# Layer boundaries that leave the trunk divided by a per-token factor, with another chain of norms; layer B's weight remainders on VectorE alone; layer C's cache loads spread out

## The chip, the cores and the metric

One of the eight cores of one Trainium2 chip. The metric is the device time of the program in microseconds (us); the shown figure is the median of three runs.

## The reference

One inference step of a four-layer encoder for 336 tokens: 64 frames of a running stream and 272 (16 meta tokens and 256 frames) of a new one. Each layer is

```
x <- x + rmsnorm(mixer(rmsnorm(x, norm_pre)), norm_post)
rmsnorm(x, g) = x * rsqrt(mean(x*x) + 1e-6) * g
```

with D_MODEL = 1024, and the mixers are A = HGRN2 recurrence, B = RG-LRU (causal convolution, two block-diagonal gates, a linear recurrence), C = latent attention with a cache of 528 rows, D = a 31-tap convolution module. Each mixer has an input projection from 1024, a SiLU gate of width 2048, and an output projection from 2048 to 1024. The outputs are the 336 rows of x after layer D and the new states of the mixers.

## The kernel before, in words

Everything lies transposed: features on the 128 partitions, the 336 tokens along the free axis, so x is 8 slices of 128x336. Every weight matrix is read once, in groups of up to 128x1024 float32, by class `Weights`: a DMA on SP's queue into one of three `wraw` buffers, a rounded part `whi` made by ScalarE (L321), and the remainder `wlo = wraw - whi` (L333) made by VectorE (DVE), or by GpSimd (POOL) for the groups that stand in `PRM["lo"]`. Of these, 26 belong to layer B (10 `bg`, 8 `bx`, 4 `bw`, and the 4 `bo1` that exist) and 38 to layer D. There are five buffers for the pairs `whi`, `wlo`. A product is three matmuls (`mm3`): whi with the rounded activations, whi with their remainder, wlo with the rounded ones.

The order of the work is the order of the Python program: each engine runs its own instructions in that order (`manual_schedule`), and the lists in `PRM` say which step of which unit comes next. `PRM["b"]` is layer B's list of steps with a lag each: a unit n is 256 of the 2048 channels, with two x tiles (`x0`, `x1`), two gate tiles (`g0`, `g1`), a convolution for each x tile (`conv0`, `conv1`, L942 and L944), `split` (rounded part and remainder of the convolved tile), `gate` (the two block-diagonal products, tile `gacc`), `decay` (L978 to L980, with a POOL square), `mult` (L985, L986), `root` (L990 to L994) and `recur` (the scan L1000, the gating L1004 and L1005, and the split into `oh`, `ol`, L415 and L416). What is left after the last g or x tile is handed out over the 16 slices of the output projection by `PRM["bt"]`.

`outproj` runs a layer's end. Its first phase goes over the 16 slices of `oh`, `ol` into MPAR accumulators (2 in A and C, 4 in B, 6 in D), its second makes the rest of the eight output slices one by one (`bacc`). `evac` takes each: the square (sums `s`), the slice times norm_post (`yg`), its square (sums `q`), and x times yg (sums `p`); POOL also makes the sums of x squared (`xsq`, L544 and L546). Four float32 matmuls with a matrix of ones (`Ss`, `Sq`, `Sp`, `Sx`) sum over the partitions. From Ss comes r = rsqrt(mean y^2 + eps) (`rstd`, L422 Ln and L423 Exp); POOL multiplies the eight `yg` slices by r (L587); the sum of squares of the new x is Sx + r (2 Sp + r Sq) (L589 to L592), and another Ln and Exp give the next layer's factor `rn`. `first_tiles` then goes over the eight slices: `upd` adds yg to x (L596), `scale` makes u = x * norm_pre * rn (L460), ScalarE rounds it to `uh` (L466) and DVE makes `ul` (L471), while TensorE runs the next layer's first four tiles (`hacc`), three matmuls for each of four tiles in every slice. `w.ahead()` and `w.get()` move the weight pipeline on.

Layer C's head (L1085 to L1093) issues ten loads (RoPE tables, pair mask, cache) on ScalarE's queue, and then evacuates four q and two kv tiles (`raw_tile`, L1119 to L1123), with POOL adding the squares.

In layer D's output projection (`ready`, L1606 to L1625) DVE normalises a slice, POOL multiplies it with its gate (L1613), ScalarE rounds it and DVE makes the remainder `ol`, two to four slices ahead of TensorE.

Of the kernel before, what the change touches and what calls it, by code (L numbers as in the profile page):

```python
# [18 lines left out]
D = 1024  # L19
# [332 lines left out]
class Trunk:  # L352
# [14 lines left out]

    def start(self):
# [61 lines left out]
    def first_norm(self):  # L430
# [5 lines left out]
        sq0 = self.nrm.tile([128, NT], F32, name="sst")  # L436
# [5 lines left out]
        self.mm(ss[:, :NT], self.ones, sq0, True, True)  # L442
        self.w.ahead()
        return self.rstd(ss[:, :NT], D)

    def first_tiles(self, i, r, upd=None):
# [5 lines left out]
        order = [(k, j) for k in range(KD) for j in range(4)]  # L452
        if upd is None:
            upd = lambda k: None
            order.sort(key=lambda z: max(2 * z[0], 3 * z[1]))
        us = {}
# [34 lines left out]
    def outproj(self, i, layer, ready, close):  # L491
# [20 lines left out]
        with ExitStack() as st:  # L512
# [29 lines left out]
            def xsq(m):  # L542
                q = new("x", m)
                G.tensor_tensor(q, self.x[:, m], self.x[:, m], op=OP.mult)  # L544
                if m:
                    G.tensor_tensor(sums["x"], sums["x"], q, op=OP.add)  # L546
# [1125 lines left out]
```

## Time and profile before

| | |
|---|---|
| runs shown | 1369.55, 1371.46, 1374.95 us (median 1371.46) |
| profiled execution | 1373.4 us; span from the first to the last instruction 1371.3 us |
| mean granted TensorE clock | 0.968 of full |
| busy in the span | TensorE 92%, weight loads 87%, DVE 70%, ScalarE 60%, POOL 34% |
| layer A, B, C, D by their first tiles | 0 to 403, 403 to 662, 662 to 1046, 1046 to 1371 us |

Times in rows are counted from the start of the span. A matmul row starts when its data may enter the array, and neighbours overlap; the distance of two starts is what one costs. L390 is the line of every matmul, so its rows are told apart by their tiles. PEld is the weight load, ACTq and POOLq the queue of an engine. "idle before" with an arrow names what ended the wait.

### The profile page before, as it was taken

To read this page: it belongs to the slowest core of one execution; us is meant where nothing else is said; L and a number is where in the kernel's file an instruction comes from. 1 tells how busy PE (TensorE), PEld (TensorE's weight loads), DVE (VectorE), ACT (ScalarE), POOL (GpSimd) and SP (SyncE) were. 2 spreads that over 40 slices of the span, in tenths; PEclk is the share of its full clock that TensorE was granted. 3 is DMA by queue.
4 is the path that set the end of the run, shared out by engine and by line. 5 is a ranking of instruction groups with operands and counts; after the bars stand their busy time and mean duration, and the time that the engine had idled before them with its cause. 6 is when DMAs were issued, how large, how long until landed. Compare 5 with 4: busy or idle time off the path is not lost.

```text
span 1371.3 us, 21204 instructions
## 1 busy us (share of the span) xinstructions
PE 1267.3 (92%) x8016; PEld 1197.1 (87%) x8016; DVE 959.6 (70%) x1683; ACT 817.6 (60%) x1554; POOL 460.4 (34%) x452
## 2 busy tenths in 40 slices
PE   5999999999979998789789999998897999999996
PEld 5999999999969988789779998887796899888895
DVE  5676666667667989876665555554856699989783
ACT  4677766666535766655364444444543878777663
POOL 0000000002245534452240000000404599999783
PEclk9999999999989999999899999999998999999998
DMA  5433334333423333234342322131242232333251
GB/s 196 142 120 109 111 120 131 111 109 108 154 93 108 109 123 112 104 123 147 110 155 76 113 92 98 63 105 50 77 144 79 93 108 98 103 116 101 95 166 41
DMA packets 48422, 151.28 MB, mean 110 GB/s; under 512 B 6432, under 2 KB 12016, under 8 KB 48320
## 3 DMA queue, kind: packets, MB, share of 16 engines
q1 hardware_dynamic: 44880, 142.70, 31.8%
q0 software_dynamic: 1392, 4.63, 1.1%
q10 hardware_dynamic: 2048, 2.60, 0.6%
q8 instruction: 63, 1.03, 0.3%
q14 instruction: 39, 0.32, 0.1%
HBM read 145.45 MB, written 4.46 MB: 109 GB/s over the span
## 4 chain that ended last, share of the span: by engine, by line
PE 59%; DVE 15%; ACT 8%; POOL 5%; issue 5%; DMA 3%; ACTq 0%; POOLq 0%; SPq 0%; DVEq 0%
PE acc L390 32%; PE bacc L390 9%; DVE xc L944 3%; POOL gp L1481 3%; PE o L390 3%; PE cv L390 3%; PE hacc L390 2%; DMA wraw<-in_wts_dram 2%; DVE wlo L333 2%; PE y L390 2%; PE sp L390 2%; ACT whi L321 2%; ACT Pp L1349 2%; PE ss L390 2%; POOL wlo L333 1%
## 5 line engine op out<-in xcount | busy, mean ns | idle before, releaser
L390 PE MATMUL acc<-uh,wlo 128*128 128x336 f32 x1208 | 385.7, 319 | 11.7 <-DVE wlo L333 7.0
L390 PE MATMUL acc<-uh,whi 128*128 128x336 f32 x1208 | 393.7, 326 | 1.1 <-ACT vv L879 1.1
L390 PE MATMUL acc<-ul,whi 128*128 128x336 f32 x1208 | 384.3, 318 | 0.0
L321 ACT ACTIVATE whi<-wraw 128x1024 fp32r<-128x1024 f32 (+2 forms) x267 | 274.1, 1028 | 108.6 <-DMA wraw<-in_wts_dram 59.2
L333 DVE TENSOR_TENSOR wlo<-wraw,whi 128x1024 fp32r<-128x1024 f32 (+2 forms) x203 | 257.6, 1281 | 38.8 <-ACT whi L321 33.8
L390 PEld LDWEIGHTS acc<-uh,wlo 128*128 128x128 f32 x1208 | 228.7, 189 | 13.6 <-DVE wlo L333 7.9
L390 PEld LDWEIGHTS acc<-uh,whi 128*128 128x128 f32 x1208 | 229.5, 190 | 3.7 <-ACT vv L879 1.6
L390 PEld LDWEIGHTS acc<-ul,whi 128*128 128x128 f32 x1208 | 229.8, 190 | 2.1
L333 POOL TENSOR_TENSOR wlo<-wraw,whi 128x1024 fp32r<-128x1024 f32 (+1 forms) x64 | 155.5, 2434 | 115.8 <-DVE sump L522 74.3
L1489 DVE SCALAR_TENSOR_TENSOR cv<-dext,dw,cv 128x366 f32<-128x366 f32 x280 | 146.2, 602 | 2.0 <-POOL gp L1481 1.4
L1481 POOL TENSOR_TENSOR gp<-gp,gq 128x366 f32<-128x366 f32 x109 | 115.8, 1063 | 27.8 <-ACT gq L1480 21.3
L544 POOL TENSOR_TENSOR sumx<-x 128x336 f32<-128x336 f32 x3 | 2.8, 949 | 326.6 <-PE x L773 326.6
L390 PE MATMUL bacc<-oh,wlo 128*128 128x336 f32 x288 | 91.4, 317 | 1.0 <-DVE wlo L333 1.0
L390 PE MATMUL bacc<-oh,whi 128*128 128x336 f32 x288 | 92.2, 320 | 0.0
L390 PE MATMUL bacc<-ol,whi 128*128 128x336 f32 x288 | 91.1, 316 | 0.0
L1480 ACT ACTIVATE gq<-dext,dw 128x366 f32<-128x366 f32 x109 | 61.8, 598 | 25.8 <-POOL gp L1481 25.4
L1198 POOL DMA_DIRECT2D uv<-in_wts_dram x8 | 5.8, 720 | 199.3 <-DVE sg L1106 116.0
L390 PE MATMUL acc<-oh,whi 128*128 128x336 f32 x192 | 63.6, 331 | 9.2 <-DVE sgb L1015 6.8
L390 PE MATMUL acc<-ol,whi 128*128 128x336 f32 x192 | 63.3, 330 | 3.5 <-DVE ol L416 3.5
L944 DVE SCALAR_TENSOR_TENSOR xc<-ext,vec,xc 128x340 f32<-128x340 f32 x48 | 62.4, 1300 | 1.7
L390 PE MATMUL acc<-oh,wlo 128*128 128x336 f32 x192 | 62.5, 325 | 0.0
L390 PE MATMUL hacc<-uh,whi 128*128 128x336 f32 x128 | 45.2, 353 | 18.1 <-ACT uh L466 18.0
(407 smaller groups left out, 2761.2 us busy)
## 6 DMA issues: line engine op xcount, KB each, us to landing
wraw<-in_wts_dram SPq DMA_DIRECT2D x243, 512.0 KB, 3.5
wraw<-in_wts_dram SPq DMA_DIRECT2D x16, 384.0 KB, 3.1
out_hg_dram<-sf SPq DMA_DIRECT2D x16, 128.0 KB, 2.0
wraw<-in_wts_dram SPq DMA_DIRECT2D x8, 256.0 KB, 2.7
ukt<-in_ukt_dram POOLq DMA_DIRECT2D x8, 256.0 KB, 3.0
uv<-in_wts_dram POOLq DMA_DIRECT2D x8, 256.0 KB, 3.8
x<-in_x_dram SPq DMA_DIRECT2D x8, 168.0 KB, 5.6
out_y_dram<-x SPq DMA_DIRECT2D x8, 168.0 KB, 1.9
```

The source lines that it names most:

```text
L321: self.nc.scalar.activation(hi[:, :n], self.raw[i][:, :n], AF.Copy)
L333: e.tensor_tensor(lo[:, :n], self.raw.pop(i)[:, :n], hi[:, :n].bitcast(F32), op=OP.subtract)
L390: self.PE.matmul(out, l, r, start=start, stop=stop)
L544: G.tensor_tensor(q, self.x[:, m], self.x[:, m], op=OP.mult)
L944: V.scalar_tensor_tensor(xc[:, t], e[:, t, j:j + T], self.col("bcw", 16 * j + c), xc[:, t], op0=OP.mult, op1=OP.add)
L1198: nc.gpsimd.dma_start(uv, src[:, :, 256 * (p % 2):256 * (p % 2) + 256])
L1349: A.activation(P[r0:r1, c:c + n], s[r0:r1, c:c + n], AF.Exp, scale=C_SCALE, bias=mx[r0:r1, j:j + 1], accum_out=sm[r0:r1, j:j + 1])
L1480: A.activation(q, e[:, n:n + T], AF.Copy, scale=tap(n, j))
L1481: G.tensor_tensor(cv[j, "p"], cv[j, "p"], q, op=OP.add)
L1489: V.scalar_tensor_tensor(c[:, :T], ext[j % NX][:, n:n + T], tap(n, j), c[:, :T], op0=OP.mult, op1=OP.add)
```

## The change

At the boundaries A to B, B to C and C to D x is no longer kept as the true x, but as x divided by a factor per token. In place of yg * r the update is x * s + yg with s = 1/r, made per slice: POOL multiplies slices 0 and 1 by s, DVE the other six, each just before its addition. The factor of the following norm is computed for that scaled x: t = (Ss + D eps) * x1 + Sq + Sp * s, where `x1` is the mean square of the x before (carried from boundary to boundary) and Sp already holds the factor 2; `w` = rsqrt(t / D). From the second boundary on, s is multiplied by `xr`, the factor that was left out before. `xr` and `x1` for the next boundary are made after the first tiles (two Exp on ScalarE, two POOL operations). The sums of x squared (`xsq`, Sx) are gone; Sq and Sp take the last slice by a second matmul instead of a DVE addition. In layer D's output projection POOL multiplies the eight x slices by `xr`, one at each even k.

In `first_tiles`, 13 matmuls of constants into an unused accumulator stand ahead of the first real one; the three products of a slice go in another order (whi and wlo with `uh` for all four tiles, then whi with `ul`); DVE's update comes after `ul`; a fifth weight group is split at slice 4.

Layer B's groups leave `PRM["lo"]`, so DVE makes all its remainders; `PRM["b"]` and `PRM["bt"]` are others. Layer C's two small tables load through POOL's queue, its eight cache loads one behind each evacuated tile and two at the end; the squares are added by DVE.

```
-    "b": [["decay", 1], ["g0", 0], ["mult", 1], ["g1", 0], ["split", 0], ["root", 1], ["x1", -1], ["x0", -2],
-         ["conv0", -1], ["gate", 0], ["recur", 1], ["conv1", -1]],
-    "bt": [0, 4, 3, 0, 12, 11, 3, 10, 2, 10, 17, 1, 24, 9],
+    "b": [["g0", 0], ["decay", 1], ["mult", 1], ["split", 0], ["g1", 0], ["root", 1], ["x1", -1], ["x0", -2],
+          ["recur", 1], ["conv0", -1], ["gate", 0], ["conv1", -1]],
+    "bt": [3, 1, 9, 13, 15, 24, 18, 9, 12, 6, 16, 17, 18, 24],
...
-    "lo": [["bg", 1], ["bg", 3], ["bg", 4], ["bg", 7], ["bg", 8], ["bg", 10], ["bg", 11], ["bg", 12], ["bg", 14],
...
+    "lo": [["da", 1], ["da", 5], ["da", 7], ["da", 8], ["da", 10], ["da", 12], ["da", 15], ["db", 1], ["db", 2],
...
@@ first_norm
+        self.x1 = self.nrm.tile([128, NT], F32, name="x1", bufs=1)
         self.w.ahead()
-        return self.rstd(ss[:, :NT], D)
+        r = self.rstd(ss[:, :NT], D)
+        self.V.tensor_scalar(self.x1, ss[:, :NT], 1.0 / D, EPS, op0=OP.mult, op1=OP.add)
+        return r
@@ first_tiles
             self.A.activation(self.uh[:, k], us[k], AF.Copy)
-            if k + 2 < KD:
-                upd(k + 2)
             if k + 1 < KD:
                 scale(k + 1)
             self.V.tensor_tensor(self.ul[:, k], us.pop(k), self.uh[:, k].bitcast(F32), op=OP.subtract)
+            if k + 2 < KD:
+                upd(k + 2)
             if self.w.ns < 4:
                 self.w.ahead()
+            if k == 4 and order is None:
+                self.w.step(4)
+        self.w.second(self.w.ns - 1)
...
+        for _ in range(idle):
+            self.mm(accs[3][:, :128], self.ident, self.ones)
+        if order is None:
+            for k in range(KD):
+                for j in range(4):
+                    h, l = ws[j]
+                    self.mm(accs[j][:, :NT], h[:, k], self.uh[:, k], k == 0, False)
+                    self.mm(accs[j][:, :NT], l[:, k], self.uh[:, k], False, False)
+                for j in range(4):
+                    self.mm(accs[j][:, :NT], ws[j][0][:, k], self.ul[:, k], False, k == KD - 1)
@@ outproj
+                if last and self.xr is not None and k % 2 == 0:
+                    G.tensor_tensor(self.x[:, k // 2], self.x[:, k // 2], self.xr, op=OP.mult)
...
-                V.tensor_tensor(p, self.x[:, m], yg[:, m], op=OP.mult)
+                V.scalar_tensor_tensor(p, self.x[:, m], 2.0, yg[:, m], op0=OP.mult, op1=OP.mult)
...
+                self.mm(S["q"], self.ones, sums["q"], True, False)
             self.mm(S["s"], self.ones, tail["s"], False, True)
...
+                self.mm(S["p"], self.ones, sums["p"], True, False)
+                for n in "qp":
+                    self.mm(S[n], self.ones, tail[n], False, True)
+                l, sq, t, w = (bp.tile([128, NT], F32, name=n) for n in ("lq", "sroot", "sst", "wz"))
+                A.activation(l, S["s"], AF.Ln, scale=1.0 / D, bias=self.eps)
+                A.activation(sq, l, AF.Exp, scale=0.5)
+                V.scalar_tensor_tensor(t, S["s"], D * EPS, self.x1, op0=OP.add, op1=OP.mult)
+                if self.xr is not None:
+                    V.tensor_tensor(sq, sq, self.xr, op=OP.mult)
+                V.tensor_tensor(t, t, S["q"], op=OP.add)
+                V.tensor_tensor(S["p"], S["p"], sq, op=OP.mult)
+                V.tensor_tensor(t, t, S["p"], op=OP.add)
+                l2 = bp.tile([128, NT], F32, name="sqq")
+                A.activation(l2, t, AF.Ln, scale=1.0 / D)
+                A.activation(w, l2, AF.Exp, scale=-0.5)
+                NG = 2
+                for k in range(NG):
+                    G.tensor_tensor(self.x[:, k], self.x[:, k], sq, op=OP.mult)
             def upd(k):
+                if k >= NG:
+                    V.tensor_tensor(self.x[:, k], self.x[:, k], sq, op=OP.mult)
                 V.tensor_tensor(self.x[:, k], self.x[:, k], yg[:, k], op=OP.add)
...
-            self.first_tiles("abcd".index(self.layers[self.layers.index(layer) + 1]), rn, upd)
+            self.first_tiles("abcd".index(self.layers[self.layers.index(layer) + 1]), w, upd, 13)
+            if self.xr is None:
+                self.xr = self.nrm.tile([128, NT], F32, name="xr", bufs=1)
+            A.activation(self.xr, l, AF.Exp, scale=-0.5)
+            A.activation(l, l, AF.Exp, scale=-1.0)
+            G.tensor_scalar(t, t, 1.0 / D, None, op0=OP.mult)
+            G.tensor_tensor(self.x1, t, l, op=OP.mult)
@@ layer_c
-            nc.scalar.dma_start(rp.rearrange("p a b -> p (a b)"), self.d["k_rope"])
-            nc.scalar.dma_start(pm.rearrange("p a b -> p (a b)"), self.d["k_pair"])
...
+            nc.gpsimd.dma_start(rp.rearrange("p a b -> p (a b)"), self.d["k_rope"])
+            nc.gpsimd.dma_start(pm.rearrange("p a b -> p (a b)"), self.d["k_pair"])
+            loads = [(keyt[:, l, a:b], self.d["ct"][:, l, c:d])
+                     for l in range(2) for a, b, c, d in ((0, 512, 0, 512), (576, NK, 512, NCACHE))]
+            loads += [(kps[:, :512], self.d["cr"][:, :512]), (kps[:, 576:], self.d["cr"][:, 512:]),
+                      (keyk[:, :4], self.d["ck"]), (keyk[64:80, 4], self.d["ckt"])]
...
-                    (G if j < 3 else V).tensor_tensor(sq, sq, q, op=OP.add)
+                    V.tensor_tensor(sq, sq, q, op=OP.add)
+                if loads:
+                    nc.scalar.dma_start(*loads.pop(0))
...
+            for z in loads:
+                nc.scalar.dma_start(*z)
```

## Rows read from the trace of the kernel before

**Rows 1.** Busy time by stretch: start:end, length, each engine (x instructions), clock, DMA.

```profile
402.80:422.50 19.70, 17.79 (x97) 17.36 (x98) 13.88 (x29) 5.97 (x13) 5.21 (x10) 0.80 0.10 29
...
471.50:475.30 3.80, 3.73 (x14) 3.73 (x15) 3.18 (x6) 3.25 (x5) 0.02 (x1) 0.56 0.72 251
...
421.00:588.00 167.00, 142.71 (x860) 138.91 (x858) 149.15 (x153) 111.19 (x177) 82.86 (x97) 0.94 0.34 115
588.00:634.00 46.00, 45.14 (x281) 44.86 (x281) 31.60 (x37) 27.67 (x40) 26.30 (x28) 0.96 0.34 111
```

**Rows 2.** Chain that ended last (start, us): 24 matmuls at the end of layer A.

```profile
390.48 3.73 PE bacc L390 x24
```

**Rows 3.** Timeline of the boundary A to B (start, us, engine, line, instruction).

```profile
389.19 0.72 PE L390 MATMUL Sx<-sumx,ones 128*128 128x336 f32 x2
389.75 0.73 PE L390 MATMUL Ss<-sums,ones 128*128 128x336 f32 x2
...
394.24 0.45 ACT L529 ACTIVATE sqs<-bacc 128x336 f32<-128x336 f32 x1 [3.94 <-PE bacc L390]
...
396.19 0.48 ACT L423 ACTIVATE rstd<-lnss 128x336 f32<-128x336 f32 x1
396.75 8.45 POOL L587 TENSOR_TENSOR yg<-yg,rstd 128x336 f32<-128x336 f32 x8 [10.44 <-ACT rstd L423]
397.74 0.51 DVE L590 SCALAR_TENSOR_TENSOR sst<-Sp,sst 128x336 f32<-128x336 f32 x1
398.28 0.58 DVE L591 TENSOR_TENSOR sst<-sst,rstd 128x336 f32<-128x336 f32 x1
...
402.78 0.65 PE L390 MATMUL hacc<-uh,whi 128*128 128x336 f32 x1 [5.23 <-ACT uh L466]
...
405.62 0.65 PE L390 MATMUL hacc<-ul,whi 128*128 128x336 f32 x1 [1.92 <-DVE ul L471]
405.91 0.56 DVE L460 SCALAR_TENSOR_TENSOR u<-x,vec,rstd 128x336 f32<-128x336 f32 x1
...
407.22 0.56 DVE L460 SCALAR_TENSOR_TENSOR u<-x,vec,rstd 128x336 f32<-128x336 f32 x1
```

**Rows 4.** Layer B, VectorE by line, 421 to 588: busy, mean ns, idle before.

```profile
L944 DVE SCALAR_TENSOR_TENSOR xc<-ext,vec,xc 128x340 f32<-128x340 f32 x48 | 62.4, 1300 | 1.7
L333 DVE TENSOR_TENSOR wlo<-wraw,whi 128x1024 fp32r<-128x1024 f32 x16 | 19.5, 1218 | 0.0
L942 DVE TENSOR_SCALAR xc<-ext,vec 128x340 f32<-128x340 f32 x16 | 19.4, 1210 | 5.5 <-ACT ext L1024 5.5
```

**Rows 5.** Instructions on tile xc: ns min/median/max.

```profile
L944 DVE SCALAR_TENSOR_TENSOR xc<-ext,vec,xc x48: 571/575/2741, 425.0 to 581.4; 128x340 f32<-128x340 f32 x48
L942 DVE TENSOR_SCALAR xc<-ext,vec x16: 450/454/2534, 422.8 to 578.7; 128x340 f32<-128x340 f32 x16
```

**Rows 6.** Layer B, POOL by line, 421 to 588.

```profile
L333 POOL TENSOR_TENSOR wlo<-wraw,whi 128x1024 fp32r<-128x1024 f32 x21 | 55.9, 2666 | 8.4 <-ACT whi L321 8.0
L980 POOL TENSOR_TENSOR w<-av 128x680 f32<-128x680 f32 x7 | 10.3, 1476 | 22.2 <-ACT av L978 22.2
```

**Rows 7.** Layer B, TensorE timeline: the first matmul behind a wait.

```profile
471.57 0.42 PE L390 MATMUL acc<-uh,wlo 128*128 128x336 f32 x1 [1.94 <-DVE wlo L333]
```

**Rows 8.** Layer C's head on ScalarE (timeline).

```profile
676.31 0.48 ACTq L1092 DMA_DIRECT2D kps<-in_cr_dram  x1
...
681.80 1.06 ACT L321 ACTIVATE whi<-wraw 128x1024 fp32r<-128x1024 f32 x1 [7.82 <-DMA keyk<-in_ckt_dram]
```

**Rows 9.** Layer D's output projection: POOL and DVE timeline.

```profile
1296.58 1.17 POOL L1613 TENSOR_TENSOR dt<-dt,dsg 128x336 f32<-128x336 f32 x1
...
1299.50 1.17 POOL L1613 TENSOR_TENSOR dt<-dt,dsg 128x336 f32<-128x336 f32 x1
...
1314.16 2.08 DVE L1625 TENSOR_TENSOR ol<-dt,oh 128x336 fp32r<-128x336 f32 x1
```

**Rows 10.** The same projection in the chain: four accumulators of slice 8.

```profile
1319.38 1.85 PE acc L390 x12
```

More of the change, by code (lines that the diff above doesn't have):

```diff
@@ L366, in __init__ @@
         self.w = Weights(tc, ctx, d["wts"], all_groups(layers))
+        self.xr = None
     def start(self):
@@ L435, in first_norm @@
         nc.scalar.preload_act_table_set(LN_SET)
-        sq0 = self.nrm.tile([128, NT], F32, name="sst")
+        sq0 = self.nrm.tile([128, NT], F32, name="u32")
         for k in range(KD):
@@ L442, in first_norm, with first_tiles @@
         self.mm(ss[:, :NT], self.ones, sq0, True, True)
+        self.x1 = self.nrm.tile([128, NT], F32, name="x1", bufs=1)
         self.w.ahead()
-        return self.rstd(ss[:, :NT], D)
-    def first_tiles(self, i, r, upd=None):
+        r = self.rstd(ss[:, :NT], D)
+        self.V.tensor_scalar(self.x1, ss[:, :NT], 1.0 / D, EPS, op0=OP.mult, op1=OP.add)
+        return r
+    def first_tiles(self, i, r, upd=None, idle=0):
         names = [g[:2] for g in layer_groups("abcd"[i])[:4]]
@@ L451, in first_tiles @@
         accs = [hp.tile([128, 512], F32, name=f"hacc{j}") for j in range(4)]
-        order = [(k, j) for k in range(KD) for j in range(4)]
         if upd is None:
             upd = lambda k: None
+            order = [(k, j) for k in range(KD) for j in range(4)]
             order.sort(key=lambda z: max(2 * z[0], 3 * z[1]))
+        else:
+            order = None
         us = {}
@@ L476, in first_tiles @@
         ws = [tuple(z.rearrange("p (k c) -> p k c", k=KD) for z in w) for w in ws]
-        for k, j in order:
-            h, l = ws[j]
-            self.mm(accs[j][:, :NT], h[:, k], self.uh[:, k], k == 0, False)
-            self.mm(accs[j][:, :NT], l[:, k], self.uh[:, k], False, False)
-            self.mm(accs[j][:, :NT], h[:, k], self.ul[:, k], False, k == KD - 1)
+        for _ in range(idle):
[8 more added lines that the diff above has]
+                    self.mm(accs[j][:, :NT], ws[j][0][:, k], self.ul[:, k], False, k == KD - 1)
+        else:
+            for k, j in order:
+                h, l = ws[j]
+                self.mm(accs[j][:, :NT], h[:, k], self.uh[:, k], k == 0, False)
+                self.mm(accs[j][:, :NT], l[:, k], self.uh[:, k], False, False)
+                self.mm(accs[j][:, :NT], h[:, k], self.ul[:, k], False, k == KD - 1)
         self.early = {n: a[:, :NT] for n, a in zip(names, accs)}
@@ L497, in outproj @@
         kg = 1024 // (128 * mp)
+        last = self.layers[-1] == layer
         accs = [self.acc() for _ in range(mp)]
@@ L510, in outproj @@
         close()
-        last = self.layers[-1] == layer
         with ExitStack() as st:
@@ L514, in outproj @@
             yg = bp.tile([128, KD, NT], F32, name="yg")
-            sums = {n: bp.tile([128, NT], F32, name="sum" + n) for n in ("s" if last else "spqx")}
+            sums = {n: bp.tile([128, NT], F32, name="sum" + n) for n in ("s" if last else "spq")}
             tail = {}
             def add(n, m, t):
-                if m == 7 and n == "s":
+                if m == 7:
                     tail[n] = t
@@ L537, in evac @@
                 p = new("p", m)
-                V.tensor_tensor(p, self.x[:, m], yg[:, m], op=OP.mult)
+                V.scalar_tensor_tensor(p, self.x[:, m], 2.0, yg[:, m], op0=OP.mult, op1=OP.mult)
                 add("q", m, q)
                 add("p", m, p)
[L542 to L546, printed above, removed]
             for m in range(mp):
@@ L552, in outproj @@
             ps = self.pool(pst, "bnd_s", 1, PSUM)
-            S = {n: ps.tile([128, 512], F32, name="S" + n)[:, :NT] for n in "sqpx"}
+            S = {n: ps.tile([128, 512], F32, name="S" + n)[:, :NT] for n in "sqp"}
             if last:
@@ L556, in outproj @@
             pa = self.pool(pst, "bnd_a", 4, PSUM, side="right")
-            todo = list(range(8))
             for m in range(mp, 8):
@@ L567, in outproj @@
                     self.w.tick()
-                    if not last and todo:
-                        xsq(todo.pop(0))
                     if m == 7 and g == 0:
-                        if not last:
-                            while todo:
-                                xsq(todo.pop(0))
-                            self.mm(S["x"], self.ones, sums["x"])
                         self.mm(S["s"], self.ones, sums["s"], True, False)
@@ L578, in outproj @@
                 evac(m, acc)
+            if not last:
+                self.mm(S["q"], self.ones, sums["q"], True, False)
             self.mm(S["s"], self.ones, tail["s"], False, True)
-            for n in S:
-                if n in "qp":
-                    self.mm(S[n], self.ones, sums[n])
-            r = self.rstd(S["s"], D)
-            if not last:
-                for k in range(KD):
-                    G.tensor_tensor(yg[:, k], yg[:, k], r, op=OP.mult)
-                t = bp.tile([128, NT], F32, name="sst")
-                V.tensor_tensor(t, S["q"], r, op=OP.mult)
-                V.scalar_tensor_tensor(t, S["p"], 2.0, t, op0=OP.mult, op1=OP.add)
-                V.tensor_tensor(t, t, r, op=OP.mult)
-                V.tensor_tensor(t, S["x"], t, op=OP.add)
-                rn = self.rstd(t, D)
+            if last:
+                r = self.rstd(S["s"], D)
+            else:
+                self.mm(S["p"], self.ones, sums["p"], True, False)
[16 more added lines that the diff above has]
+                    G.tensor_tensor(self.x[:, k], self.x[:, k], sq, op=OP.mult)
             def upd(k):
+                if k >= NG:
+                    V.tensor_tensor(self.x[:, k], self.x[:, k], sq, op=OP.mult)
                 V.tensor_tensor(self.x[:, k], self.x[:, k], yg[:, k], op=OP.add)
```

7 lines of the change are left out of this document (removed), and 27 rows, old and new, of the table PRM.

## The prediction

> **What bounds the kernel now.** I began with busy time by stretch, looking for stretches in which TensorE has idle time or a low clock. In most of A, C and D it works without a break. Two kinds of stretch are left. The first is the three boundaries: the 96 matmuls of the first tiles take 19.7 us at A to B, at a mean granted clock of 0.80 [rows 1]; the same view gives 19.5 and 19.0 us at the two others, at 0.81 and 0.84. At full clock (the 2.4 GHz level) 24 matmuls take 3.73 us [rows 2], 0.155 us each, so 96 would take 14.9. The timeline of one boundary shows why: TensorE waits 5.23 us for the first `uh` and 1.92 us more for the first `ul`, and the matmuls behind these waits are of double length, 0.65 us [rows 3]: the 1.2 GHz level. The second is layer B's main part, 421 to 588: TensorE has 860 matmuls there, 133.7 us at 0.155, and takes 167 us, while VectorE (DVE) is busy for 149.2 of them [rows 1]. By line, the convolution's steps are what fills DVE: 48 on L944 with a mean of 1300 ns, 16 on L942 with a mean of 1210 [rows 4]. By tile, half of them take 575 and 454 ns, and the longest 2741 and 2534 [rows 5]. The excess is about one POOL remainder long (2666 ns [rows 6]). Behind B's main part, 588 to 634, TensorE is busy for 45.1 of 46 us [rows 1]; there a faster DVE is worth nothing.
>
> **The change: boundaries.** I count from the end of A's last output slice, where ScalarE starts its square at 394.24 [rows 3]. The old way to the first real matmul is 8.54 us, to 402.78.
>
> The new chain splits in two. ScalarE still makes Ln and Exp of Ss, so s is there at 396.67, when `rstd` is there now (396.19 + 0.48). On TensorE three float32 sums follow the Ss tail, each 0.56 us (389.19 to 389.75), so Sp ends at about 397.0. The two operations on DVE that need Sp are dependent, and a dependent pair starts 0.54 us apart (397.74 to 398.28) [rows 3], so t is there at about 398.3, and Ln and Exp (two of about 0.5, and the hand-overs) give w at 399.4. At the second and third boundary s * xr comes ahead of these: 0.5 us more, w at 399.9.
>
> The slices do not wait for w alone. POOL multiplies slices 0 and 1 from 396.8 or 397.3 on, at 8.45 / 8 = 1.06 us each [rows 3], to 398.9 or 399.45, and DVE's two additions behind it (0.42 and 0.5) end at 399.85 or 400.4. That is late by 0.5 us against w. With u, `uh` and the hand-overs (1.2 us) the first real matmul starts at 401.0 or 401.6, earlier by 1.75, 1.2 and 1.2 us: **4.15 us**.
>
> The 13 constant matmuls lie in that wait. A float32 matmul of 336 columns costs 0.56 us, so I estimate 128 columns at 0.21, and 13 at 2.8 us: from 397.0 to 399.8. They end before `uh` is there and cost nothing. If they were left out, the wait would be 4.0 to 4.6 us. What they leave is 1.2, 1.8 and 1.8 us of idle time in place of 5.23. Layer B shows what the longer of these may cost: behind a wait of 1.94 us [rows 7] the clock was 0.56 for 3.8 us, with 14 matmuls [rows 1] that need 2.2 at full clock, 1.6 us lost. I count that once, for the two longer waits together: **+1.6**.
>
> DVE now has four operations in a slice in place of three. A slice takes 1.31 us now (405.91 to 407.22 [rows 3]); one more operation that depends on the one ahead adds 0.54, and the next u, which now depends on its direct neighbour, 0.12: 1.97 us. TensorE needs 12 x 0.155 = 1.86 us for a slice. It starts 1.4 us behind the first `u` and three slices are under way by then, so DVE's 0.11 per slice uses up most of the lead by slice 7, and no more. The first `ul` comes 0.5 us behind the first `uh`, covered by eight matmuls. So the tiles take 14.9 us in place of 19.7, 19.5 and 19.0: **13.5 us**. Sx no longer stands between the last products, 0.56 us each time: **1.7 us**. The terms give 19.4 - 1.6 = 17.8; I take **-17.5**, since the next layer's first evacuation now stands behind two more Exp on ScalarE (0.48 each), most of it covered by the fifth tile (3.7 us). POOL's 16 operations for x squared lie beside a TensorE without a break and are worth nothing by themselves.
>
> **Layer B.** DVE gets 21 more remainders in the main part, at 1.218 us [rows 4, 6]: +25.6. If the convolution's steps go to their medians, they fall from 62.4 to 27.6 and from 19.4 to 7.3 [rows 4, 5]: -46.9. Not all of this goes: POOL's seven squares (1476 ns [rows 6]) stay and can each hold one step up for about 1 us: +7. Net -14.3. DVE is idle for 17.9 us in 421 to 588 and I leave that as it is. So the main part falls from 167 to about **153 us, -14**. From below it is bounded by TensorE's 134 us and its hand-overs, say 142: -25. From above, by medians that are not reached: if half of the 46.9 stays, DVE ends at +9. I take the value near the medians, because the step beside no POOL work is the commoner one. The four `bo1` remainders (5 us on DVE) fall into 588 to 634, where DVE is busy for 31.6 of 46 us [rows 1], and cost nothing; with a late DVE each would cost 1.2.
>
> That the excess comes from POOL is what the rows suggest, no more: the longest step is a median step and 2166 ns, less than a remainder of 2666 [rows 5, 6]. The Trainium skill ("SBUF — State Buffer", Who interferes with whom) says that a DVE instruction with two SBUF inputs and a GpSimd instruction that reads SBUF lock each other out for a whole instruction. By that rule the slower case below, which needs long steps without POOL's remainders, could not come, while layer D, where `ol` has two SBUF inputs, would pay for each of POOL's new operations in full; that is a rival of its own.
>
> **Layer C's head.** ScalarE waits until 681.80 behind its ten loads [rows 8], while the first tiles end at about 682. A gain is bounded by one late evacuation, some 1 us, and by 5 us if the chain behind it all moves up; a loss by eight issues of 0.48 us [rows 8] that now stand between evacuations, 3.8. DVE's additions replace POOL's on a DVE that is idle. I take **-1**.
>
> **Layer D's output projection.** POOL gets eight multiplications of 1.06 us. A slice of POOL's gate and remainder takes 2.92 us now (1296.58 to 1299.50 [rows 9]), a slice of TensorE 18 x 0.155 = 2.79, so POOL has no room at first. But DVE is ahead: the `ol` of slice 8 ends at 1316.24 [rows 9] and TensorE takes it at 1319.38 [rows 10], 3.1 us later. Four or five additions before that slice make 5 us, and some come back where DVE makes the remainders. Between 0 and 8.5 us; I take **+1**.
>
> The start's extra DVE operation lies beside Ln and Exp, and the fifth weight group's rounding between two `uh` on a ScalarE that is idle for 0.8 us a slice: nothing.
>
> **Sum:** -17.5 - 14 - 1 + 1 = -31.5. The profiled execution took 1373.4 us (span 1371.3), 0.14% above the median of 1371.46. So 1341.9 for it, and **1340** beside the median. About 0.5% is what a measurement of this kernel can tell from no change.
>
> **Rivals.**
>
> *Layer B only changes hands.* DVE takes the remainders, and its waits on ScalarE and POOL grow by what the long steps give back; `decay` now stands behind `g0`, so the square that L986 needs comes later. For it: ScalarE and DVE hand work to each other in every unit. Against: DVE's idle time is 17.9 us, small beside the excess. Then 1371.5 - 17.5 = 1354.
>
> *Layer B reaches TensorE's bound.* With 142 us in the main part it is 11 us better: 1329.
>
> *The clock still falls as before.* Of the 13.5 us, three waits of 1.92 us for `ul` make 5.8; the other 7.7 are the low clock and come back if the constants do not hold it, less the 1.6 counted: 1346. For it: the fall behind 1.94 us [rows 7]. Against: the three waits are shorter than that.
>
> *POOL paces layer D's end.* Each of eight new operations holds POOL for 1.06 us, and DVE's `ol` as long (2.08 us in place of 0.5 [rows 9]); beyond the lead of 3.1 us some 5 are left in place of 1: 1344. This is the rule of the Trainium skill's SBUF page (same section) at work; the long `ol` agrees with it.
>
> *DVE becomes the chain of layer B: slower.* The place is 421 to 588. If the long steps are not POOL's doing, 25.6 us of remainders are pure addition; and if L986 waits in seven units for Exp, Tanh and the square (some 3.6 us behind `g0`'s evacuation, of which DVE fills 1.3), 16 more. The main part grows by 42, against 17.5 gained: 1371.5 + 42 - 17.5 - 1 + 1 = 1396. It decides from the point where the long steps give back less than 24 of their 46.9 us.
>
> *It does not do what it says.* The chain is no shorter, because s and POOL's two slices hold the additions, and B changes hands: 1367 or so.
>
> **How the numbers follow.** The forecast has a chance of 0.46 (its own range 1329 to 1351), layer B changing hands 0.14, TensorE's bound 0.12, the clock 0.09, POOL in D 0.07, slower 0.07, no effect 0.05. All but the last two are faster by over 0.5%: 0.88, 0.05 and 0.07. The range takes in 1329 less the 5 us that layer C could give and the 6 that B's main part lies above TensorE's 134 us below, and 1354 with the 7 of a late layer D above: **1318 to 1361**.
>
> **What would show it.** Right: the first-tile stretches at a clock near 1.00 and about 15 us long; first real matmul 6.8 to 7.4 us behind the last square; L944's mean near 700 ns and the main part near 153 us. Wrong: a row of doubled matmul length behind the constants; a wait of DVE on POOL at L986 or of TensorE on DVE's `wlo` in B; TensorE waiting for `ol` in D. The forecast fails if DVE in B is busy for more than 150 us again.

## The result, and the profile after

The changed kernel takes **1332.12 us** (median of 4 runs, 1329.06 to 1332.71) beside 1370.99 of the kernel before: a ratio of 0.9708, 95% interval 0.9682 to 0.9733. That is 39 us less; the forecast was 1340 (1318 to 1361). Its profiled execution took 1332.71 us with a span of 1330.9. The page's first part, busy time by engine:

```profile
PE 1261.2 (95%) x8100; PEld 1194.0 (90%) x8100; DVE 932.3 (70%) x1727; ACT 818.8 (62%) x1560; POOL 339.6 (26%) x376
```

By stretch (start:end, length, busy time with the count of instructions for TensorE, weight loads, VectorE, ScalarE and POOL in this order, then clock, DMA share, GB/s): the constant matmuls (two records for each of the 13), the first tiles at the three boundaries, and layer B from behind its first tiles to its first `bacc` matmul.

```profile
397.50:400.30 2.80, 2.80 (x26) 2.78 (x25) 2.49 (x6) 0.96 (x2) 2.11 (x3) 1.00 0.00 0
401.00:416.00 15.00, 14.90 (x96) 14.80 (x97) 13.65 (x28) 4.55 (x10) 0.00 (x0) 1.00 0.00 1
633.00:648.00 15.00, 15.00 (x97) 14.90 (x98) 13.53 (x27) 4.54 (x9) 0.00 (x0) 1.00 0.01 1
1004.00:1021.30 17.30, 15.43 (x96) 14.72 (x97) 14.82 (x26) 4.39 (x9) 3.94 (x2) 1.00 0.10 31
416.00:595.60 179.60, 169.68 (x1059) 167.97 (x1058) 152.36 (x206) 132.52 (x206) 35.63 (x93) 0.96 0.42 139
```

The tiles that took 19.7 us at a clock of 0.80 [rows 1] take 14.9 at 1.00, except at C to D, where TensorE is busy for only 15.4 of 17.3 us. The chain at A to B, from the timeline (start, duration, engine, line), which answers to [rows 3]:

```profile
394.65 0.45 ACT L551 ACTIVATE sqs<-bacc 128x336 f32<-128x336 f32 x1 [3.37 <-PE bacc L389]
...
396.59 0.48 ACT L602 ACTIVATE sroot<-lq 128x336 f32<-128x336 f32 x1
...
397.16 1.75 POOL L614 TENSOR_TENSOR x<-x,sroot 128x336 f32<-128x336 f32 x2 [393.15 <-ACT sroot L602]
...
398.34 0.51 DVE L608 TENSOR_TENSOR sst<-sst,Sp 128x336 f32<-128x336 f32 x1
...
399.45 0.48 ACT L611 ACTIVATE wz<-sqq 128x336 f32<-128x336 f32 x1
...
401.10 0.42 PE L389 MATMUL hacc<-uh,whi 128*128 128x336 f32 x1 [0.52 <-ACT uh L472]
```

From the last square to the first real matmul it is 6.45 us in place of 8.54. The convolution's steps in layer B, by tile (ns min/median/max), answer to [rows 5]; not one is longer than its median by 5 ns:

```profile
L973 DVE SCALAR_TENSOR_TENSOR xc<-ext,vec,xc x48: 571/573/577, 423.8 to 552.0; 128x340 f32<-128x340 f32 x48
L971 DVE TENSOR_SCALAR xc<-ext,vec x16: 449/452/455, 423.3 to 550.3; 128x340 f32<-128x340 f32 x16
```

Where the 40.4 us between the two profiled spans come from is seen when each trace is cut at the starts of the same matmuls: first and last of the first tiles (`hacc`), first of the out-projection (`acc` on `oh`), first and last `bacc`. The two columns on the right are experiments told below: the new boundaries alone, and the new layer B alone, on the kernel before. Differences of some us in "C behind them" say little: that stretch varies by up to 5 us without an edit in layer C (run 7 and the last section).

| stretch, us | before | after | difference | boundaries alone | B alone |
|---|---|---|---|---|---|
| start to A's last `bacc` | 393.88 | 394.29 | +0.4 | 393.05 | 393.80 |
| A to B: to the first tile matmul | 8.89 | 6.81 | -2.1 | 6.81 | 8.88 |
| first tiles of B | 19.49 | 14.86 | -4.6 | 18.30 | 19.81 |
| B behind them, to its first `bacc` | 199.45 | 179.63 | **-19.8** | 205.83 | 175.41 |
| B's `bacc` | 31.92 | 30.07 | -1.9 | 30.07 | 30.63 |
| B to C: to the first tile matmul | 8.90 | 7.25 | -1.7 | 7.25 | 8.89 |
| first tiles of C | 19.32 | 14.87 | -4.5 | 14.86 | 18.63 |
| C behind them, to its out-projection | 288.45 | 288.20 | -0.3 | 290.62 | 284.47 |
| C's out-projection, to its first `bacc` | 21.28 | 16.02 | **-5.3** | 16.03 | 21.32 |
| C's `bacc` | 45.48 | 44.90 | -0.6 | 44.90 | 45.48 |
| C to D: to the first tile matmul | 8.89 | 6.99 | -1.9 | 6.99 | 8.89 |
| first tiles of D | 18.81 | 17.31 | -1.5 | 18.29 | 18.67 |
| D behind them, to its out-projection | 226.13 | 229.24 | **+3.1** | 229.84 | 226.09 |
| D's out-projection to the end | 80.45 | 80.50 | 0.0 | 80.68 | 80.44 |

### The profile page after: what moved, and what is told of

It reads as the page before. It is cut to its first block, busy times and chain, and to the rows that moved or that the text cites. A ratio compares the mean times of both kernels' runs of the same rounds, so it can differ in the third digit from the quotient of the medians.

```text
span 1330.9 us, 21343 instructions
## 1 busy us (share of the span) xinstructions
PE 1261.2 (95%) x8100; PEld 1194.0 (90%) x8100; DVE 932.3 (70%) x1727; ACT 818.8 (62%) x1560; POOL 339.6 (26%) x376
## 4 chain that ended last, share of the span: by engine, by line
PE 60%; DVE 11%; ACT 9%; POOL 9%; issue 5%; DMA 2%; POOLq 0%; DVEq 0%; ACTq 0%
PE acc L389 33%; PE bacc L389 10%; POOL gp L1511 5%; PE o L389 3%; PE hacc L389 3%; DVE wlo L330 2%; POOL wlo L330 2%; PE y L389 2%; ACT whi L318 2%; PE sp L389 2%; DMA wraw<-in_wts_dram 2%; ACT Pp L1379 2%; PE ss L389 2%; PE misc L389 1%; PE x L389 1%
## 5 line engine op out<-in xcount | busy, mean ns | idle before, releaser
L330 DVE TENSOR_TENSOR wlo<-wraw,whi 128x1024 fp32r<-128x1024 f32 (+2 forms) x229 | 288.0, 1272 | 32.9 <-ACT whi L318 28.3
L614 POOL TENSOR_TENSOR x<-x,sroot 128x336 f32<-128x336 f32 x6 | 5.2, 893 | 448.6 <-ACT sroot L602 393.1
L330 POOL TENSOR_TENSOR wlo<-wraw,whi 128x1024 fp32r<-128x1024 f32 (+1 forms) x38 | 88.9, 2345 | 102.9 <-DVE sump L544 83.2
L389 PE MATMUL cv<-dext,diag 128*128 128x366 f32 x182 | 59.0, 472 | 1.0 <-ACT diag L1484 0.9
L1379 ACT ACTIVATE Pp<-sp,mx 64x80 f32<-64x80 f32 (+4 forms) x80 | 30.0, 376 | 45.9 <-DVE mx L1377 26.0
```

The costliest lines, as they stand in the source:

```text
L330: e.tensor_tensor(lo[:, :n], self.raw.pop(i)[:, :n], hi[:, :n].bitcast(F32), op=OP.subtract)
L389: self.PE.matmul(out, l, r, start=start, stop=stop)
L614: G.tensor_tensor(self.x[:, k], self.x[:, k], sq, op=OP.mult)
L1379: A.activation(P[r0:r1, c:c + n], s[r0:r1, c:c + n], AF.Exp, scale=C_SCALE, bias=mx[r0:r1, j:j + 1], accum_out=sm[r0:r1, j:j + 1])
```

## The experiments

Twelve kernels in three sets, each set beside runs of the kernel before on its own chip; times are medians, ratios are to those runs. Code lines shift by a few between kernels.

**1. Layer B's remainders back on POOL.** The new order of the steps stays.

```diff
-    "lo": [["da", 1], ["da", 5], ["da", 7], ["da", 8], ["da", 10], ["da", 12], ["da", 15], ["db", 1], ["db", 2],
...
+    "lo": [["bg", 1], ["bg", 3], ["bg", 4], ["bg", 7], ["bg", 8], ["bg", 10], ["bg", 11], ["bg", 12], ["bg", 14],
...
+          ["bx", 7], ["bx", 12], ["bx", 15], ["da", 1], ["da", 5], ["da", 7], ["da", 8], ["da", 10], ["da", 12],
...
```

> The changed kernel with layer B's 26 remainders given back to POOL; the new order of layer B's steps stays. Theory 1 (POOL's remainders stretch the convolution's steps on DVE): the mean of the 48 multiply-add steps goes from 573 ns back above 1100, and the stretch from the last first-tile matmul of layer B to its first bacc matmul from 179.6 us to 195 to 205, so 1347 to 1357 us in all. Theory 2 (the new order of the steps made the gain): the steps stay below 700 ns, DVE has less to do than in the changed kernel, the stretch is within 5 us of 179.6: 1327 to 1337 us.

1358.68 us, ratio 0.9905 (0.9886 to 0.9924): 26.6 more than the changed kernel and 1.7 above the range of theory 1. The stretch behind the first tiles went from 179.6 to 201.6 us, as theory 1 has it, but the steps' mean came only to 787 ns, not above 1100. VectorE (DVE) and POOL by line in that stretch (busy, mean ns | idle before):

```profile
L976 DVE SCALAR_TENSOR_TENSOR xc<-ext,vec,xc 128x340 f32<-128x340 f32 x48 | 37.8, 787 | 1.7
L333 DVE TENSOR_TENSOR wlo<-wraw,whi 128x1024 fp32r<-128x1024 f32 x23 | 30.1, 1313 | 6.1 <-ACT whi L321 6.1
L1032 DVE TENSOR_TENSOR_SCAN h<-av,vec,ti 128x340 f32<-128x340 f32 x16 | 26.7, 1707 | 0.8 <-POOL ti L1026 0.8
L1018 DVE SCALAR_TENSOR_TENSOR w<-w,tz 128x680 f32<-128x680 f32 x8 | 15.6, 1948 | 3.2 <-POOL w L1012 3.2
...
L333 POOL TENSOR_TENSOR wlo<-wraw,whi 128x1024 fp32r<-128x1024 f32 x23 | 62.6, 2720 | 18.7 <-ACT whi L321 14.2 <-PE acc L392 4.5
```

In the new order other operations stand beside the remainders, and those are held (their own rows grow longer): the scans take 1707 ns (907 in the changed kernel), `w` 1948 (857). What is held depends on the order, how much does not.

**2. The old order, remainders on DVE.**

```diff
-    "b": [["g0", 0], ["decay", 1], ["mult", 1], ["split", 0], ["g1", 0], ["root", 1], ["x1", -1], ["x0", -2],
-          ["recur", 1], ["conv0", -1], ["gate", 0], ["conv1", -1]],
-    "bt": [3, 1, 9, 13, 15, 24, 18, 9, 12, 6, 16, 17, 18, 24],
+    "b": [["decay", 1], ["g0", 0], ["mult", 1], ["g1", 0], ["split", 0], ["root", 1], ["x1", -1], ["x0", -2],
+         ["conv0", -1], ["gate", 0], ["recur", 1], ["conv1", -1]],
+    "bt": [0, 4, 3, 0, 12, 11, 3, 10, 2, 10, 17, 1, 24, 9],
```

> The changed kernel with layer B's steps in the order of before (both lists); the remainders stay on DVE. Theory 1 (POOL's remainders): steps near 600 ns, the stretch from the last first-tile matmul to the first bacc matmul within 5 us of 179.6, so 1328 to 1338 us. Theory 2 (the order): that stretch goes to 195 or more, so 1347 us or more.

1334.43 us, ratio 0.9729 (0.9713 to 0.9745); the stretch is 182.7 us. The order is worth 3.1 us in the trace and 2 in the time, which the intervals do not separate.

**3. Layer B wholly as before**, edits 1 and 2 together.

> The changed kernel with layer B wholly as before (order and remainders). Both theories: the stretch goes back to about 199.5 us and the time to 1350 to 1356. What it adds: if layer B and the rest are separate, this run and the run before differ by the boundaries, C and D alone, that is by 16 to 20 us.

1362.13 us, ratio 0.9929 (0.9906 to 0.9952): only 9.6 below the kernel before, not 16 to 20. Layer B's stretch is now 205.4 us, 6 *longer* than in the kernel before. Nearly all of the 6 lie ahead of DVE's first step of the convolution: from that step to the first `bacc` it is 199.6 us here and 198.9 in the kernel before. The windows of the stretch, first of run 2, then of this run (columns as above):

```profile
414.20:596.90 182.70, 170.05 (x1059) 167.19 (x1058) 155.04 (x206) 132.11 (x204) 42.68 (x93) 0.97 0.40 134
```

```profile
417.00:622.40 205.40, 177.34 (x1058) 173.41 (x1058) 172.00 (x180) 131.21 (x204) 93.41 (x117) 0.93 0.33 116
```

The same two by line, the remainders on DVE:

```profile
L330 DVE TENSOR_TENSOR wlo<-wraw,whi 128x1024 fp32r<-128x1024 f32 x46 | 56.6, 1245 | 5.6 <-ACT whi L318 5.4
```

```profile
L333 DVE TENSOR_TENSOR wlo<-wraw,whi 128x1024 fp32r<-128x1024 f32 x23 | 27.9, 1218 | 3.4 <-ACT whi L321 3.4
```

DVE's other work is 155.0 - 56.6 = 98.4 us without POOL's 23 remainders and 172.0 - 27.9 = 144.1 with them: **2.0 us of DVE for each remainder that POOL takes**, where DVE itself needs 1.22. The new order gives the same 2.0: 152.4 - 55.4 = 97.0 in the changed kernel, 173.0 - 30.1 = 142.9 in run 1.

**4. POOL's squares of x back**, summed as before, the sum unused.

```diff
+            if not last:
+                sumx = bp.tile([128, NT], F32, name="sumx")
+
+            def xsq(m):
+                q = bp.tile([128, NT], F32, name="sqx") if m else sumx
+                G.tensor_tensor(q, self.x[:, m], self.x[:, m], op=OP.mult)
+                if m:
+                    G.tensor_tensor(sumx, sumx, q, op=OP.add)
...
+                    if not last and todo:
+                        xsq(todo.pop(0))
...
```

> The changed kernel with POOL's 8 squares of x and 7 additions put back at each of the three layer ends; their sum is used by nothing. Theory 1 (POOL stretches DVE's operations that lie beside it): the ten or more `ol` splits at layer C's end go from 0.44 to about 1.0 us each, TensorE waits for them again, layer C's out-projection (first acc matmul on oh to first bacc matmul) goes from 16.0 to 20 to 22 us, and the time to 1336 to 1342 us. Theory 2 (as the forecast had it: beside a TensorE without a break they are worth nothing): 1330 to 1334 us, that stretch stays at 16 us.

1340.82 us, ratio 0.9773 (0.9739 to 0.9807): theory 1. Layer C's out-projection took 21.3 us again. There, DVE and POOL by line, and then TensorE's waits (us in total, times, longest):

```profile
L415 DVE TENSOR_TENSOR ol<-sg,oh 128x336 fp32r<-128x336 f32 x16 | 14.4, 957 | 0.0
...
L571 POOL TENSOR_TENSOR sumx<-sumx,sqx 128x336 f32<-128x336 f32 x7 | 8.1, 1152 | 0.5
```

```profile
PE acc L389 <- DVE ol L415: 3.1, 3, 1.6
```

DVE is busy for 20.3 of those 21.3 us, and the mean granted clock there is 0.92, in the changed kernel's out-projection 1.00: the waits are 3.1 of the 5.3 us, the lower clock costs most of the rest. The changed kernel's `ol` in the same place, with POOL idle:

```profile
L415 DVE TENSOR_TENSOR ol<-sg,oh 128x336 fp32r<-128x336 f32 x16 | 7.0, 503 | 0.1
```

**5. No constant matmuls** (13 becomes 0 in the call of `first_tiles`).

> The changed kernel without the 13 constant matmuls at each boundary (they feed nothing). Theory 1 (they keep TensorE's granted clock up over the wait): without them the three first-tile stretches run at a mean clock near 0.8 again and take 16.5 to 18.5 us instead of 14.9, 14.9 and 17.3, so 1336 to 1342 us. Theory 2 (the chain is short enough by itself): the stretches stay within 0.3 us and the time is 1330 to 1334.

1330.80 us, ratio 0.9708 (0.9673 to 0.9744): no change in the time that these runs can tell. The first tiles take 16.3, 16.3 and 17.3 us, so neither theory held as a whole:

```profile
401.00:417.50 16.50, 16.50 (x101) 16.50 (x100) 12.87 (x26) 5.54 (x10) 0.00 (x0) 0.92 0.11 33
632.50:649.00 16.50, 16.50 (x99) 16.50 (x98) 12.89 (x26) 5.21 (x9) 0.00 (x0) 0.90 0.09 33
1001.00:1019.00 18.00, 17.62 (x100) 16.92 (x101) 14.95 (x26) 5.07 (x9) 3.97 (x2) 0.91 0.08 30
```

The clock falls without them, as theory 1 has it, but to 0.90 to 0.92 and not to 0.8. That costs 1.4 us at each of the first two boundaries and nothing at the third, where TensorE waits anyway. Those 2.8 us do not show in the total: A's first tiles were 1.3 us shorter in this execution and the stretch of C 2.9, stretches that vary without any edit in them.

**6. The fifth weight group of layer D on DVE** (`["db", 2]` leaves the list). In the changed kernel's timeline at C to D:

```profile
1011.47 2.66 POOL L330 TENSOR_TENSOR wlo<-wraw,whi 128x1024 fp32r<-128x1024 f32 x1 [9.41 <-ACT whi L318]
1011.83 2.67 DVE L475 TENSOR_TENSOR ul<-u,uh 128x336 fp32r<-128x336 f32 x1
...
1014.55 0.73 PE L389 MATMUL hacc<-ul,whi 128*128 128x336 f32 x3 [1.73 <-DVE ul L475]
```

> The changed kernel with one remainder of layer D (that of the fifth weight group, rounded during the first tiles) on DVE instead of POOL. Theory 1 (this POOL operation holds the `ul` beside it): the first-tile stretch at C to D goes from 17.3 to 14.9 us, no `ul` there is longer than 0.6 us, and the time to 1328 to 1331. Theory 2 (the wait comes from DVE's four operations in a slice, 1.97 us against TensorE's 1.86): the stretch stays above 16.5 us and the time at 1331 to 1334.

1329.84 us, ratio 0.9694 (0.9664 to 0.9724). The stretch is 14.86 us, theory 1, though the time by itself is not told apart from the changed kernel's; all eight `ul` take 0.5:

```profile
L475 DVE TENSOR_TENSOR ul<-u,uh 128x336 fp32r<-128x336 f32 x8 | 4.0, 503 | 0.2
```

**7. Layer C's loads all at once on ScalarE's queue**, as before.

> The changed kernel with layer C's ten loads again issued all at once on ScalarE's queue. Theory 1 (they held ScalarE's evacuations; the shorter boundary makes it worse): the stretch from layer C's last first-tile matmul to its out-projection goes from 288.2 to 291 to 294 us, and the time to 1335 to 1338. Theory 2 (the head is held by the chain through DVE behind them): within 1 us of 288.2, 1331 to 1334 us.

1336.54 us, ratio 0.9737 (0.9703 to 0.9771), 4.4 above the changed kernel, but the intervals of the two overlap; the stretch is 292.0 us. The waits in C's head (who waited for whom: us in total, times, longest), and ScalarE's first evacuation there, then the same one in the changed kernel:

```profile
PE misc L389 <- DVE qsq L1153: 7.9, 1, 7.9
ACT whi L318 <- DMA keyt<-in_ct_dram: 7.7, 1, 7.7
```

```profile
657.90 0.43 ACT L1149 ACTIVATE qr<-hacc 128x336 f32<-128x336 f32 x1
```

```profile
650.48 0.43 ACT L1145 ACTIVATE qr<-hacc 128x336 f32<-128x336 f32 x1
```

Theory 1. Neither the time nor the whole stretch decides it: among the ten kernels that have the new loads the stretch lies between 284.9 and 290.3 us without an edit in layer C. Its head does, from the last first-tile matmul to the first `sp` matmul: 50.7 to 53.3 us in those ten, 56.4 here, and 56.5 in run 11, which has the old loads behind the new boundary too. With the old loads behind the old boundary it is 51.5 (the kernel before) and 50.3 (run 12).

**8. The factor on x at the start of D**, where POOL is idle, with run 6's edit; the next x1 is not prepared at this boundary.

```diff
-                if last and self.xr is not None and k % 2 == 0:
-                    G.tensor_tensor(self.x[:, k // 2], self.x[:, k // 2], self.xr, op=OP.mult)
...
+                for k in range(KD):
+                    G.tensor_tensor(self.x[:, k], self.x[:, k], self.xr, op=OP.mult)
```

> As the run with the fifth remainder on DVE, and POOL's eight multiplications of x by the factor stand at the start of layer D, where POOL is idle for 8 us (1023 to 1032 in the changed kernel's trace), instead of in its out-projection; at this boundary the preparation of the next boundary's x1 is left out, since nothing uses it. Theory 1 (in the out-projection they hold DVE's `ol`, 1.2 us in waits of TensorE): that stretch goes from 50.4 to 48.5 to 49.3 us, the main part of D stays at 229 to 230, and the time is 1326 to 1330. Theory 2 (POOL sets the pace of D's main part, so 8 us more at its start are paid there): the main part goes to 232 or more, and the time to 1331 or more.

1331.00 us, ratio 0.9696 (0.9664 to 0.9728): nothing won over run 6. The out-projection fell from 50.4 to 49.6 us, less than expected, and TensorE no longer waits for its late `ol`. D's main part grew to 233.0, theory 2's number, but not by its mechanism: the first convolution stood behind the multiplications, through POOL's clearing of its buffers.

```profile
PE cv L389 <- POOL dext L1468: 3.5, 1, 3.5
```

**9. The same, behind the clearing of the buffers** (the loop of run 8 stands after the memsets).

> As factor_early, but POOL's eight multiplications stand behind its memsets of layer D's convolution buffers, so that TensorE's first convolution does not wait for them (3.55 us at 1025 in factor_early). Theory 1 (that wait was the loss): D's stretch behind the first tiles goes from 233.0 back to 229 to 230, the out-projection stays at 49.6, and the time is 1325 to 1329. Theory 2 (POOL's own load in D's main part is the limit, and 8 us more are paid later): the stretch stays at 232 or more, 1329 to 1332 us.

1324.95 us, ratio 0.9642 (0.9619 to 0.9664), D's main part 229.3 us, its out-projection 49.5: theory 1 (0.05 us under its range); its interval lies below the changed kernel's. Of the 6 us to run 8 the trace has 3.7 in D's main part and 3.9 in C's, which has no edit.

**10. Three more remainders on DVE** (`db` 5, `db` 14, `dg` 5). This stands on run 9. In the changed kernel TensorE waited in D's main part:

```profile
PE acc L389 <- POOL wlo L330: 5.1, 3, 2.0
```

> As factor_behind, and three of layer D's remainders that TensorE waited for (db 5, db 14, dg 5) on DVE instead of POOL. Theory 1 (POOL is late there, DVE has room): TensorE's waits for POOL's remainders, some 4 to 5 us in D's main part, fall below 1, and the time to 1322 to 1326. Theory 2 (DVE, busy for nine tenths of D's main part, becomes the one that is late): the stretch stays at 229 or grows, 1326 to 1332.

**1323.37 us**, ratio 0.9633 (0.9610 to 0.9655), the best of all. The wait is 0.6 us, D's main part 225.2 (229.3 in run 9), its out-projection 48.0. From run 9 the time alone does not separate it.

**11. The boundaries alone** on the kernel before.

> The new boundaries alone on the kernel before: layer B (order, remainders) and layer C's loads as before. Theory 1 (the boundaries' term stands by itself, as the forecast summed it): 1371 - 17.5 + 1, that is 1353 to 1358 us. Theory 2 (what the boundary gives is given back behind it: by a layer B whose chain is DVE, which gets more operations in the first tiles, and by layer C's head behind its loads): the first tiles are 14.9 to 17.3 us as in the changed kernel, but the stretch of layer B behind them grows from 199.5 to some 205 and that of C from 288.4 to some 292, and the time is 1363 to 1370 us.

1364.64 us, ratio 0.9931 (0.9908 to 0.9954): 8 us, theory 2 (column of the table). The tiles took 18.3 us at A to B and at C to D, outside what was expected: a remainder on POOL stands beside them at A to B too, 2.66 us long at 407.44, with an `ul` of 2.67 at 407.79.

**12. Layer B alone** on the kernel before.

> The new layer B alone (order, remainders) on the kernel before. Theory 1 (layer B's gain stands by itself, as large as it was when it was undone): 1371 - 30, that is 1338 to 1344 us. Theory 2 (part of it needs the new boundary, since there it also takes back what the boundary would have lost): the stretch behind B's first tiles falls from 199.5 to 180 to 184 and the time to 1350 to 1356 us. The forecast's term of 14 by itself would give 1357.

1344.51 us, ratio 0.9788 (0.9765 to 0.9810): 28 us, theory 1 (0.5 above its range); layer B's own two stretches have 25.3 of them in the trace. The stretch behind the first tiles fell to 175.4, below what theory 2 had: with the old boundary in front, it is 4.2 us shorter than in the changed kernel.

## Why the prediction was right, and where it was not

The total is within 8 us of the forecast, the parts are not. Alone, layer B gives 28.4 us (run 12) where the forecast had 14; the boundaries give 8.3 (run 11) where it had 17.5 less 1 in layer D; the loads give some 4 (run 7) where it had 1. The sum of the three, 41, is about the 39 measured, which is all that intervals of some 3 us on each can say. Layer B gave 14 more than forecast and the boundaries 8 less: that the total came so near is in part luck.

**The wait at the boundary** was right: 6.45, 6.90 and 6.64 us from the last square to the first matmul, forecast 6.8, 7.4 and 7.4. POOL's two multiplications took 1.75 us, not 2.1, and so did not hold the additions. The 13 constants took 2.80 us, as estimated. The fall of the clock counted at 1.6 us did not come, and the rival that all of the old low clock stays is out: even without any constants it costs 2.8 (run 5).

**The first tiles** were right at two boundaries (14.9 us; a slice of DVE takes 1.98 us, forecast 1.97). At C to D the step that failed is "the fifth weight group's rounding between two `uh` ...: nothing". It costed ScalarE's part alone; the group's remainder is POOL's, and held one `ul` for 2.67 us (run 6 takes 2.4 us back in that stretch).

**What lies behind the boundary** was the larger miss. The forecast took those stretches as unchanged, so that what TensorE gains is kept. In run 11 the stretches of B, C (with the old loads) and D behind the first tiles grew by 6.4, 2.2 and 3.7 us. The 2.2 is within what C's stretch varies by; D is told below. For B the trace shows how. First the changed kernel at the start of layer B, then run 3 (old layer B behind the new boundary), then run 12 (old boundary):

```profile
417.95 1.00 POOL L648 TENSOR_TENSOR x<-sst,lq 128x336 f32<-128x336 f32 x1 [17.30 <-ACT lq L646]
418.09 1.05 DVE L953 TENSOR_SCALAR spt<-vec 128x16 f32<-128x16 f32 x1
...
419.38 0.22 ACT L955 ACTIVATE sp<-sp 128x16 f32<-128x16 f32 x1 [1.58 <-DVE sp L954]
...
420.70 0.20 ACT L1052 ACTIVATE ext<-hacc 128x64 f32<-128x64 f32 x1
...
423.31 0.45 DVE L971 TENSOR_SCALAR xc<-ext,vec 128x340 f32<-128x340 f32 x1
```

```profile
423.22 2.39 POOL L333 TENSOR_TENSOR wlo<-wraw,whi 128x1024 fp32r<-128x1024 f32 x1
423.30 2.51 DVE L974 TENSOR_SCALAR xc<-ext,vec 128x340 f32<-128x340 f32 x1 [1.28 <-POOL ext L1053]
```

```profile
425.04 0.45 DVE L939 TENSOR_SCALAR xc<-ext,vec 128x340 f32<-128x340 f32 x1
```

The last line of each is DVE's first step of the convolution. In the kernel before it starts at 422.80 [rows 5]. So TensorE leaves the first tiles at 415.96 in place of 422.26, and DVE starts layer B no earlier: with four operations in a slice it is done with the tiles at 414.1, in the kernel before at 413.7. Then come two more Exp on ScalarE, and POOL's product for x1, beside which DVE's small `spt` takes 1.05 us in place of 0.17. ScalarE waits for what follows from `spt` and evacuates the first tile at 420.70, 4.7 us behind the tiles; in run 12 it does so at their end (422.42). From DVE's first step to the first `bacc` the boundary changes little: 172.3 us in the changed kernel and 172.9 in run 12, 198.9 in the kernel before, 199.6 in run 3 and 200.0 in run 11. Of a layer whose chain is DVE, the gain at the boundary is mostly lost. I had costed the Exp at 0.3 us and the slice's fourth operation for TensorE's tiles alone, and neither for the engines that start the next layer.

**Sx** was right as to its matmul: 0.57 us off the `bacc` chains of A and C. "POOL's 16 operations for x squared lie beside a TensorE without a break and are worth nothing by themselves" was wrong. They stretched `ol` to 957 ns, and layer C's out-projection paid 5.3 us; run 4 puts exactly that back. This is the largest piece of what the boundaries' part gives.

**Layer B.** The mechanism was right (the long steps were POOL's doing, and go to their medians) and its size was off. The slower rival, with long steps that stay, is out. The 860 matmuls of the main part take 144.8 us (forecast 153), and DVE is busy for 132.7 of them, not for the 150 that was to be the sign of failure:

```profile
414.70:559.50 144.80, 136.72 (x860) 135.29 (x859) 132.69 (x185) 112.65 (x181) 32.00 (x84) 0.97 0.41 135
```

"POOL's seven squares ... +7" measured 4.3, and on another operation: eight products `ti` take 1394 ns each, where the like product `w` takes 857.

```profile
L1014 DVE SCALAR_TENSOR_TENSOR ti<-ti,xc 128x680 f32<-128x680 f32 x8 | 11.1, 1394 | 0.0
```

In the old order of the steps (run 2) the squares hold the convolution's steps instead (703 ns in place of 573), by 6.2 us in all. Not in the sum were other held operations (`ol` 3.1 us over eight) and the order (3 us). DVE's busy time in the stretch fell by 20.8 us (173.2 to 152.4), the stretch by 19.8. What a remainder cost on POOL is the better number: 2.0 us of DVE, so moving it to DVE saves 0.8, and 23 of them 18. That B only changes hands is out; nearest came the rival that B reaches TensorE's bound, with 142 us for the main part. Of the signs of being wrong, DVE's wait for POOL's square ahead of `w` (2.9 us, 1.2 before) and TensorE's for a remainder of DVE (1.8 us, 7.0 before) are small. The rule of the Trainium skill ("SBUF — State Buffer", Who interferes with whom) on DVE instructions with two SBUF inputs agrees with these rows: `ul` held for 2.67 us beside a POOL operation of 2.66, `ol` 957 ns in place of 503. Had the forecast applied it to every POOL operation removed and added, as it did for layer D alone, it would have found x squared and the fifth group.

**Layer C's loads.** The forecast's "-1", with 5 as its bound, came nearer to that bound: 4.4 us in the time, 3.1 to 5.7 in the head (run 7). In run 7 the loads queue behind the boundary's last Exp on ScalarE, when the first tiles are already done; with the new boundary the old way was dearer than in the kernel before, which shows in TensorE's 7.9 us wait. So the new loads win nothing over the kernel before: they avoid what the new boundary would have cost. In the changed kernel the head is as long as before (51.5 us), and TensorE waits there 3.6 us for `sg` and 2.8 for `kvr` (2.0 and 2.2 before), both from DVE; what would shorten those was not tried.

**Layer D's end.** "+1" for the out-projection was near: it is unchanged in length, with 1.2 us of waits for `ol`, and run 8 puts the price of the eight operations there at 0.8. POOL does not pace it, and that rival is out. But D's main part lost 3.1 us, not foreseen: TensorE's waits for POOL's remainders rose from 2.8 to 5.1 us (run 10 shows the second). In the kernel before:

```profile
PE acc L390 <- POOL wlo L333: 2.8, 2, 1.7
```

Run 10 removes the waits and gains 4 us there. Why they rose behind the new boundary was not tried and stays open.

## What to carry to other kernels

Price an operation on POOL by what it does to DVE beside it: here a remainder of 1.22 us on DVE cost DVE 2.0 when POOL did it, and an operation that "fills an idle engine" cost 5 us at another place. A stretch made shorter for one engine is gained only if the engine that starts the next stretch is earlier too: look for the first instruction of that engine behind it. And where parts of a change are summed, run each of them alone once: a total can be right with both halves wrong.

## What the runs showed that I had not expected

Which DVE operation is held is a matter of order, the sum is not: 2.0 us for each remainder in either order (runs 1 and 3). Held were also operations with one tensor input: the convolution's first step, a `tensor_scalar`, took 2.51 us in place of 0.45 (run 3). The same section of the Trainium skill says that `tensor_scalar` can take the shared pair in its two-port modes; the trace agrees as far as that it was held, beside a POOL remainder of 2.39 us. In which mode it ran, no row shows.

Stretches without an edit vary with the clock: layer C's main part took 288.4 us in the kernel before and 284.5 in run 12, which leaves layer C as it was, with the same work and at a mean granted clock of 0.98 and 0.99:

```profile
681.90:970.30 288.40, 274.15 (x1776) 249.31 (x1775) 155.01 (x372) 141.18 (x353) 31.48 (x49) 0.98 0.29 92
```

```profile
656.10:940.50 284.40, 269.90 (x1776) 245.51 (x1775) 155.09 (x372) 140.66 (x353) 31.78 (x49) 0.99 0.29 93
```

So a gain of some 3 us was read here from the stretch in which it was made, not from the total, and in layer C from its head alone.
